# A hybrid decoder step on one core: the norms' sums of squares added up by VectorE in place of GpSimd

## The chip, the cores and the metric

The kernel runs on one core of one Trainium2 chip. The metric is the device time of one execution in microseconds, lower is better; the time before is a median of three runs. The core has a matrix engine (TensorE, PE in the profile, with its weight loads as PEld), three engines for element-wise work (VectorE is DVE, ScalarE is ACT, GpSimd is POOL), and DMA queues, most of them issued by SyncE (SP). Every engine executes its own list of instructions in order and waits on semaphores for the others.

## The reference, cut to what matters

Two layers of a decoder act on 512 prompt tokens and 32 sample tokens of width 1024, all in float32. Every sub-layer starts with an RMS norm and ends with a residual add:

```python
def rms_norm(x, g):
    xf = x.astype(jnp.float32)
    y = xf * lax.rsqrt(jnp.mean(xf * xf, axis=-1, keepdims=True) + RMS_EPS)
    return (y * g.astype(jnp.float32)).astype(x.dtype)
...
    for l in range(DEPTH):
        hp = rms_norm(xp, norm_mix[l])
        # even l: one projection, Mamba-2 heads (whose output is normed too) and window attention
        # odd l: forgetting attention
        ...
        xp = xp + cross_attn(rms_norm(xp, norm_xa[l]), mk, mv, w_xq[l], w_xo[l])
        xp = xp + swiglu(rms_norm(xp, norm_ffn[l]), w_ffn_in[l], w_ffn_out[l])
    y_prompt = rms_norm(xp, norm_final)
```

The sample tokens go the same way. The memory tokens of the cross-attention have a norm of their own. The step also returns states and caches.

## The kernel before, in words

Activations lie transposed: 128 features on the partitions, 8 tiles `k` of features, 544 tokens along the free axis. The tokens are worked in two chunks, `CH`: chunk 0 has 256 tokens, chunk 1 has 288 (256 prompt tokens and the 32 samples). Matrix products keep float32 accuracy by splitting every operand into a high half (a cast on ScalarE, L169, L253, L258) and a low half (a subtraction on VectorE, L170, L256, L259); three matmuls of high and low halves make one product (`acc3`, issued at L138). Weights come through SyncE's queue (L165), and a weight piece feeds 24 matmuls of each chunk. FFN inputs use a second product (L1632) on combined operands built by `operands` and `factors`.

A norm is spread over the projection that ends the sub-layer before. When TensorE has finished one output tile of one chunk, VectorE adds it from PSUM onto the residual `x` (L323; L751 and L752 in the even layer's output projection). Then `norm_tile` makes the high and low halves of `x` times the gain, without the norm's factor, ScalarE squares the tile (L264 for the first tile, straight into the accumulator `acc`; L267 for the others, into one of two `sq` buffers), and GpSimd adds the square onto `acc` (L268). There are seven such adds for each chunk of a norm. After the last tile of a chunk, `rstd` sums `acc` over the partitions with small matmuls against ones, VectorE scales and adds epsilon (L302), GpSimd raises to the power of -1/2 (L303), TensorE spreads the result over the partitions, and VectorE copies it to `b` (L310). The factor `b` is applied only when a product leaves PSUM (L457, L751, L1664 and others), or, in the FFN, when `operands` builds its inputs (L1558).

The line L268 serves seven norms: the norm in front of each cross-attention, of each FFN and of layer 1, the norm of the Mamba output (`gate`, L913), and the final norm, whose last square goes into a tile of its own, `lastsq` (L282), summed by a second matmul; that norm therefore has six adds for each chunk. 6 by 14 and 12 make 96 adds. The first norm of layer 0 (L429) and the memory norm (L1363) do not use this function: their adds stand on VectorE already. The final scaling is L1808, with the stores of `y` behind it (L1811).

In the Mamba scan (`ssm`) GpSimd also works on E (L873), the state (L901), weighted inputs (L854) and outputs (L895), and VectorE on L870, L853, L883 and others; chunk 0 of the Mamba norm falls into it.

The order of the instructions on each engine is laid out by a planner: the program is built under

```python
    with tile.TileContext(nc, schedule_with_timeline_sim=True, auto_bufs=True) as tc, ExitStack() as ctx:
```

so that the program text sets priorities, and the planner's own cost of every instruction decides what comes next on an engine. Some orders are set by hand with `after`, and interleaved by generators in `even` and `odd`.

Of the kernel before, what the change touches and what calls it, by code (L numbers as in the profile page):

```python
# [15 lines left out]
ALU = mybir.AluOpType  # L16
# [90 lines left out]
class Net:  # L107
# [153 lines left out]
    def square_acc(self, acc, src, k, N):  # L261
        nc = self.nc
        if k == 0:
            nc.scalar.activation(acc, src, AF.Square)  # L264
        else:
            sq = self.pers.tile([P, 288], F32, tag="sq", bufs=2, name=self.nm("sq"))
            nc.scalar.activation(sq[:, 0:N], src, AF.Square)  # L267
            nc.gpsimd.tensor_tensor(acc, acc, sq[:, 0:N], ALU.add)  # L268

    def norm_tile(self, st, src, k, c):  # L270
        o, N = CH[c]
# [1650 lines left out]
```

## Time and profile before

| | |
|---|---|
| median of three runs | 1657.58 us (1655.66 to 1658.09) |
| the profiled execution | 1655.56 us |
| its span, first to last instruction | 1653.8 us |
| mean granted TensorE clock | 0.993 |
| TensorE busy | 1623.4 us |
| VectorE busy | 1195.5 us |
| ScalarE busy | 795.2 us |
| GpSimd busy | 310.6 us |
| the 96 adds of L268 on GpSimd | 84.8 us |

Busy times are sums of instructions on one engine; they overlap between engines. A row of a group gives the line, the engine, the operation with its tiles, the count, then busy microseconds, the mean nanoseconds of one, and how long the engine idled just before, with what ended that idling. A row of the time line gives start, length, engine, line and tiles. A row of waits gives who waited for whom, the total, how often, and the longest.

### The profile page before, as it was taken

To read this page: it belongs to the slowest core of one execution; us is meant where nothing else is said; L and a number is where in the kernel's file an instruction comes from. 1 tells how busy PE (TensorE), PEld (TensorE's weight loads), DVE (VectorE), ACT (ScalarE), POOL (GpSimd) and SP (SyncE) were. 2 spreads that over 40 slices of the span, in tenths; PEclk is the share of its full clock that TensorE was granted. 3 is DMA by queue.
4 is the path that set the end of the run, shared out by engine and by line. 5 is a ranking of instruction groups with operands and counts; after the bars stand their busy time and mean duration, and the time that the engine had idled before them with its cause. 6 is when DMAs were issued, how large, how long until landed. Compare 5 with 4: busy or idle time off the path is not lost.

```text
span 1653.8 us, 32422 instructions
## 1 busy us (share of the span) xinstructions
PE 1623.4 (98%) x12720; PEld 1518.6 (92%) x12720; DVE 1195.5 (72%) x2327; ACT 795.2 (48%) x1629; POOL 310.6 (19%) x482
## 2 busy tenths in 40 slices
PE   8999999999999999999999999998999999999998
PEld 7999999878998999999999996656989999999997
DVE  6788789888777877777767478546567986767754
ACT  5467545444445444444435266435445444444434
POOL 0022333763322300000002113111313200000002
PEclk9999999999999999999999999999999999999999
DMA  5221334138342232323213433555441322323222
GB/s 194 65 65 52 123 111 161 40 128 290 119 170 73 66 133 87 106 81 111 86 69 138 143 112 119 173 170 178 147 179 54 122 101 77 115 84 103 77 74 84
DMA packets 71221, 189.27 MB, mean 114 GB/s; under 512 B 7612, under 2 KB 34012, under 8 KB 63452
## 3 DMA queue, kind: packets, MB, share of 16 engines
q1 hardware_dynamic: 69932, 185.43, 33.8%
q8 instruction: 100, 1.64, 0.4%
q10 hardware_dynamic: 1056, 1.24, 0.3%
q0 software_dynamic: 80, 0.52, 0.1%
q14 instruction: 53, 0.43, 0.1%
HBM read 172.22 MB, written 14.95 MB: 113 GB/s over the span
## 4 chain that ended last, share of the span: by engine, by line
PE 73%; DVE 2%; ACT 1%; issue 1%; DMA 0%; POOL 0%; POOLq 0%; DVEq 0%; SPq 0%; ACTq 0%
PE ps L138 48%; PE ps L1632 23%; PE ps L141 2%; DMA fr<-wfi 0%; DVE split_t L170 0%; DVE xn L1573 0%; POOL prt L1210 0%; ACT prt L1198 0%; DVE prt L1197 0%; ACT prt L1321 0%; DVE xf L1568 0%; DVE PT L1180 0%; DVE xpr L1473 0%; ACT split_t L169 0%; ACT PT L1180 0%
## 5 line engine op out<-in xcount | busy, mean ns | idle before, releaser
L138 PE MATMUL ps<-xh,split_t 128*128 128x288 f32 (+1 forms) x2304 | 463.2, 293 | 8.2 <-ACT split_t L169 7.8
L138 PEld LDWEIGHTS ps<-xh,split_t 128*128 128x128 f32 x2304 | 371.0, 190 | 11.2 <-ACT split_t L169 7.8
L1632 PE MATMUL ps<-xf,split_t 128*128 128x272 f32 x2592 | 350.5, 289 | 0.2 <-ACT split_t L1605 0.2
L138 PE MATMUL ps<-xl,split_t 128*128 128x256 f32 (+1 forms) x1152 | 337.9, 294 | 0.0
L1632 PEld LDWEIGHTS ps<-xf,split_t 128*128 128x128 f32 x2592 | 335.7, 188 | 1.1 <-DVE split_t L1606 0.8
L268 POOL TENSOR_TENSOR room<-room,sq 128x256 f32<-128x256 f32 (+1 forms) x96 | 84.8, 888 | 782.4 <-ACT sq L267 781.0
L138 PEld LDWEIGHTS ps<-xl,split_t 128*128 128x128 f32 x1152 | 218.6, 190 | 1.1 <-issue 0.4
L138 PE MATMUL ps<-hh,fs 128*128 128x256 f32 (+1 forms) x1024 | 208.3, 288 | 0.0
L169 ACT CAST split_t<-room 128x1024 fp32r<-128x1024 f32 (+1 forms) x128 | 130.3, 1019 | 136.3 <-PE ps L138 108.3
L170 DVE TENSOR_TENSOR split_t<-room,split_t 128x1024 fp32r<-128x1024 f32 (+1 forms) x128 | 163.8, 1282 | 26.9 <-ACT split_t L169 26.1
L1605 ACT CAST split_t<-fr 128x1024 fp32r<-128x1024 f32 x108 | 113.6, 1052 | 113.2 <-PE ps L1632 49.4
L138 PEld LDWEIGHTS ps<-hh,fs 128*128 128x128 f32 x1024 | 165.7, 188 | 0.0
L1606 DVE TENSOR_TENSOR split_t<-fr,split_t 128x1024 fp32r<-128x1024 f32 x108 | 133.0, 1231 | 42.7 <-ACT split_t L1605 40.0
L138 PE MATMUL ps<-hl,fs 128*128 128x256 f32 (+1 forms) x512 | 147.2, 288 | 0.0
L138 PE MATMUL ps<-oh,split_t 128*128 128x288 f32 (+1 forms) x512 | 102.0, 294 | 0.0
L138 PEld LDWEIGHTS ps<-hl,fs 128*128 128x128 f32 x512 | 96.4, 188 | 0.0
L138 PEld LDWEIGHTS ps<-oh,split_t 128*128 128x128 f32 x512 | 81.6, 190 | 1.8 <-issue 1.8
L138 PE MATMUL ps<-ol,split_t 128*128 128x288 f32 (+1 forms) x256 | 75.3, 295 | 0.0
L138 PE MATMUL ps<-hh,split_t 128*128 128x256 f32 (+1 forms) x384 | 73.5, 289 | 0.0
L1606 DVE TENSOR_TENSOR fs<-fr,fs 128x512 fp32r<-128x512 f32 x36 | 24.9, 691 | 65.1 <-ACT fs L1605 65.1
L258 ACT ACTIVATE xh<-x,room 128x256 fp32r<-128x256 f32 (+1 forms) x96 | 48.1, 517 | 48.9 <-DVE x L323 28.6
L1677 ACT CAST fs<-room 128x512 fp32r<-128x512 f32 x64 | 39.7, 620 | 65.0 <-PE ps L138 56.1
(428 smaller groups left out, 3150.2 us busy)
## 6 DMA issues: line engine op xcount, KB each, us to landing
fr<-wfi SPq DMA_DIRECT2D x36, 1024.0 KB
room<-wfo SPq DMA_DIRECT2D x64, 256.0 KB
room<-wo_e SPq DMA_DIRECT2D x16, 512.0 KB
xk<-mem_k SPq DMA_DIRECT2D x8, 1024.0 KB
xv<-mem_v SPq DMA_DIRECT2D x8, 1024.0 KB
room<-wfi SPq DMA_DIRECT2D x16, 512.0 KB
fox_k<-fox_k SPq DMA_DIRECT2D x64, 128.0 KB
fox_v<-fox_v SPq DMA_DIRECT2D x64, 128.0 KB
```

Source lines behind the costliest of these rows:

```text
L138: return self.placed(self.nc.tensor.matmul(out, lhsT, rhs, start=start, stop=stop))
L141: return self.placed(self.nc.tensor.transpose(out, in_, self.ident[0:k, 0:k]))
L169: nc.scalar.copy(hi[:, 0:n], raw[:, 0:n])
L170: nc.vector.tensor_tensor(lo[:, 0:n], raw[:, 0:n], hi[:, 0:n].bitcast(F32), ALU.subtract)
L258: nc.scalar.activation(hh, src, AF.Copy, scale=g)
L268: nc.gpsimd.tensor_tensor(acc, acc, sq[:, 0:N], ALU.add)
L1605: nc.scalar.copy(hi, t)
L1606: nc.vector.tensor_tensor(lo, t, hi.bitcast(F32), ALU.subtract)
L1632: self.nc.tensor.matmul(ps, w[a][:, k], x[:, b, k], start=start and k == 0 and i == 0, stop=k == 3 and i == 2, skip_group_check=True)
L1677: nc.scalar.copy(hi, raw)
```

## The change

The add of a square onto the accumulator moves from GpSimd to VectorE. The square stays on ScalarE, and the buffers stay as they are.

```diff
@@ def square_acc(self, acc, src, k, N):
         else:
             sq = self.pers.tile([P, 288], F32, tag="sq", bufs=2, name=self.nm("sq"))
             nc.scalar.activation(sq[:, 0:N], src, AF.Square)
-            nc.gpsimd.tensor_tensor(acc, acc, sq[:, 0:N], ALU.add)
+            nc.vector.tensor_tensor(acc, acc, sq[:, 0:N], ALU.add)
```

## The prediction

> **What bounds the kernel now.** I read the page first: its busy shares, its chain, and the group of the instruction that is moved.
>
> ```profile
> span 1653.8 us, 32422 instructions
> ...
> PE 1623.4 (98%) x12720; PEld 1518.6 (92%) x12720; DVE 1195.5 (72%) x2327; ACT 795.2 (48%) x1629; POOL 310.6 (19%) x482
> ...
> PE 73%; DVE 2%; ACT 1%; issue 1%; DMA 0%; POOL 0%; POOLq 0%; DVEq 0%; SPq 0%; ACTq 0%
> ...
> L268 POOL TENSOR_TENSOR room<-room,sq 128x256 f32<-128x256 f32 (+1 forms) x96 | 84.8, 888 | 782.4 <-ACT sq L267 781.0
> ```
>
> TensorE is busy for 98% of the span and carries the chain; the 96 adds are 84.8 us of GpSimd's work, and GpSimd is busy for 19%. So an add matters only where TensorE, or VectorE on its behalf, waits for it. The second view is who TensorE waited for in the whole span, the third who waited for the moved line.
>
> ```profile
> engine line waited for: us in total, times, longest us
> PE ps L138 <- ACT split_t L169: 8.2, 2, 7.8
> ...
> PE ps L138 <- DVE E L870: 1.3, 1, 1.3
> ...
> PE ps L138 <- POOL col L303: 1.0, 1, 1.0
> ...
> PE ps L138 <- ACT lastsq L282: 0.8, 1, 0.8
> ...
> PE ps L138 <- DVE xdt L853: 0.6, 1, 0.6
> ```
>
> ```profile
> who waited for it (us, times):
>   DVE oe L751: 0.7, 1
>   ACT sq L267: 0.5, 1
> ```
>
> TensorE never waited for L268. Its waits are the start (7.8 us), two VectorE results in the state-space scan (1.3 and 0.6 us), the final norm (1.0 and 0.8), and small ones in the odd layer. The reason is in the code: a norm's factor is applied when a projection leaves PSUM, so the projection runs on while the sum is still being made.
>
> **The change part by part.** *Removed:* 96 GpSimd adds (84.8 us). GpSimd's next bound disappears with them: nothing else of the norms runs there but the power L303. *Added:* 96 VectorE adds of the same shapes. The kernel has this very add on VectorE in two places:
>
> ```profile
> L429 DVE TENSOR_TENSOR room<-room,sq x14: 418/436/462, 15.4 to 31.1; 128x256 f32<-128x256 f32 x7, 128x288 f32<-128x288 f32 x7
> L1363 DVE TENSOR_TENSOR kv<-kv,sq x7: 409/410/1002, 270.5 to 288.8; 128x256 f32<-128x256 f32 x7
> 516.14 1.07 DVE L323 TENSOR_TENSOR x<-x,ps 128x256 f32<-128x256 f32 x3
> ```
>
> One add is 0.41 to 0.46 us long; three of the like in a row take 1.07 us, so a row of them costs 0.36 each. 96 by 0.43 is 41 us more of VectorE's busy time, or 35 us packed. *Given back:* VectorE's low-half splits L259 were long while GpSimd added. The groups of 522 to 541 us, and two places without a GpSimd add beside them:
>
> ```profile
> L259 DVE SCALAR_TENSOR_TENSOR xl<-x,room,xh 128x288 fp32r<-128x288 f32 x8 | 6.4, 794 | 0.2 <-ACT xh L258 0.2
> L259 DVE SCALAR_TENSOR_TENSOR xl<-x,room,xh 128x256 fp32r<-128x256 f32 x4 | 2.9, 718 | 0.0
> ...
> 525.21 0.51 DVE L259 SCALAR_TENSOR_TENSOR xl<-x,room,xh 128x288 fp32r<-128x288 f32 x1
> ...
> 455.23 3.50 DVE L259 SCALAR_TENSOR_TENSOR xl<-x,room,xh 128x256 fp32r<-128x256 f32 x7
> ```
>
> 794 against 510 ns and 718 against 500: 8 by 0.284 and 4 by 0.218 make 3.1 us that this stage gets back. That GpSimd is the cause is my inference from the times. The Trainium skill (GPSIMD Engine Reference, section Specifications) says that GpSimd shares its SBUF interfaces with VectorE and contends with VectorE instructions that have two SBUF inputs; the trace agrees, since L259 (two SBUF inputs) is long and L323 (one input from PSUM) is not. That rule also speaks against the change, because the new add has two SBUF inputs itself.
>
> Now stage by stage: VectorE busy in it, and the adds that land in it.
>
> ```profile
> core 0: us, PE busy (x) PEld busy (x) DVE busy (x) ACT busy (x) POOL busy (x), PEclk, DMA share, GB/s
> 300.00:345.00 45.00, 43.09 (x360) 38.13 (x359) 37.19 (x73) 20.29 (x51) 38.69 (x49) 1.00 0.12 36
> ...
> 522.00:541.00 19.00, 19.00 (x156) 19.00 (x155) 17.61 (x29) 14.77 (x29) 11.03 (x12) 1.00 0.31 89
> 1258.00:1276.00 18.00, 18.00 (x149) 18.00 (x148) 15.24 (x26) 12.03 (x26) 12.12 (x13) 1.00 0.41 117
> ```
>
> ```profile
> core 0: us, POOL busy (x), PEclk, DMA share, GB/s
> 300.00:345.00 45.00, 5.33 (x7) 1.00 0.12 36
> ...
> 522.00:541.00 19.00, 10.75 (x11) 1.00 0.31 89
> ```
>
> (1) *Output projections in front of the two FFNs (522 and 1258 us).* 11 adds by 0.36 are 4.0 us, less 3.1 given back: 0.9 us net in a stretch where VectorE has almost no idle time. Who needs it next:
>
> ```profile
> 536.40 0.47 DVE L259 SCALAR_TENSOR_TENSOR xl<-x,room,xh 128x256 fp32r<-128x256 f32 x1
> ...
> 537.87 0.50 PE L138 MATMUL ps<-room 128*128 128x1 f32 x4
> 538.23 0.36 PE L138 MATMUL ps<-xl,split_t 128*128 128x256 f32 x1
> ```
>
> The last split of chunk 0 ends at 536.87 and its matmul starts at 538.23, 1.36 us of cover. The sum's matmul at 537.87 stands ahead of it in TensorE's queue and will need the last VectorE add: 536.87 + 0.41 = 537.28, a cover of 0.6 us. 0.9 less 0.6 leaves 0.3, twice: +0.6. Ends: 0 (the adds fill idle time before 522), and 11 by 0.43 with nothing given back, less 0.6, that is 4.1 each or +8.2 for both.
>
> (2) *Chunk 1 of the state-space norm.*
>
> ```profile
> 411.61 1.96 DVE L259 SCALAR_TENSOR_TENSOR xl<-xs,room,xh 128x288 fp32r<-128x288 f32 x3
> ...
> 414.09 3.33 DVE L259 SCALAR_TENSOR_TENSOR xl<-xs,room,xh 128x288 fp32r<-128x288 f32 x5
> ...
> 417.48 0.40 PE L138 MATMUL ps<-xl,split_t 128*128 128x288 f32 x1
> ```
>
> VectorE ends at 417.42 and TensorE takes the last one at 417.48: no cover. The eight splits take 5.3 us, and 8 by 0.51 would be 4.1: 1.2 back, against 7 adds by 0.36 = 2.5. Net +1.3 at most, -0.3 at best; the later adds can stand behind the splits, so I take +0.5.
>
> (3) *Scan, chunk 0 of that norm (300 to 345 us).* Seven adds: 2.9 us at 0.41, 7.0 if each runs at the 1002 ns of L1363. GpSimd is busy for 38.69 of 45 us here, of which only 5.33 go, and VectorE is already held up beside it:
>
> ```profile
> 314.66 4.98 DVE L913 SCALAR_TENSOR_TENSOR xs<-zs,xs 128x256 f32<-128x256 f32 x4 [0.73 <-POOL xs L895]
> 319.56 1.27 DVE L853 TENSOR_TENSOR xdt<-ps,dt 128x512 f32<-128x512 f32 x2
> ...
> 336.28 5.30 DVE L170 TENSOR_TENSOR split_t<-room,split_t 128x1024 fp32r<-128x1024 f32 x1 [0.41 <-ACT split_t L169]
> ```
>
> These lie in front of TensorE's two waits (0.6 us on L853 and 1.3 us on L870). VectorE idles for 7.8 us of the 45, which takes most of the seven. I take +0.6 (one or two adds ahead of L853); ends -1.9 (both waits go) and +7.0.
>
> (4) *Final norm.*
>
> ```profile
> 1642.17 0.74 POOL room L268
> ...
> 1641.93 2.08 DVE L1808 TENSOR_TENSOR x<-x,ps 128x576 f32<-128x576 f32 x3 [0.64 <-PE ps L138]
> ...
> 1644.26 0.42 DVE L323 TENSOR_TENSOR x<-x,ps 128x256 f32<-128x256 f32 x1 [0.25 <-PE ps L138]
> ```
>
> The last add must now share VectorE with the three scalings of chunk 1 (to 1644.01) and the residual add at 1644.26: 0.41 less the 0.25 between them, +0.1 to +0.2, behind it the square, the sum, the power and the store. Ends -0.3 (0.74 against 0.43) and +0.4. I take +0.1.
>
> (5) *The other norms* (425 to 482, 876 to 916, 1150 to 1200 us): VectorE has slack and TensorE waits for nothing of them; 0, hidden by the projections. Without that cover a norm costs its net VectorE time, about 14 by 0.43 = 6.0 us.
>
> (6) *The wait that is added:* VectorE's add waits for ScalarE's square, and residual adds, weight splits L170 and activation splits L259 stand behind it; TensorE's PSUM banks and operands hang on those. And ScalarE's square waits, with two buffers, for VectorE's add two tiles back, with ScalarE's high halves L258 and weight casts L169 behind it. Before, this second wait was 0.5 us in all. I book 0 beyond (1) to (3), since the planner lays both lists out with these costs in view.
>
> **Sum.** 0.6 + 0.5 + 0.6 + 0.1 = +1.8 us. The profiled execution took 1655.56 us (span 1653.8 and 1.8 around it), so it would become 1657.4. It lies 2.0 under the median of the three runs (1657.58); on that median the forecast is 1659.4, +0.11%. About 0.2% (3.3 us) is what a measurement can tell from no change, so I call it no change.
>
> **The rivals.** *VectorE becomes late (slower).* If the long L259 are not GpSimd's doing, or the adds block on ScalarE's squares for as long as they would save, stage (1) costs up to 4.1 us twice; with (2) and (3) that is +9.4: 1667. Half of it is 1662. It decides from 1.4 us of TensorE idle time in each FFN entry. For it: VectorE's 17.61 of 19 us. Against: VectorE's 1195.5 us over the span leave room, and the residual adds have several PSUM banks in hand.
>
> *The shorter chain pays (faster side, yet within the bound).* An add of 0.43 instead of 0.89 us ends each norm sooner, and without GpSimd beside it the scan's waits go: -1.9, -0.3 and -0.3 give 1655.1. The Trainium skill (GPSIMD Engine Reference, section Engine selection) would send elementwise adds to VectorE, with GpSimd about twice as slow for two inputs. By that the norms' chains shorten, and the chain view bears out only 0.74 us of L268.
>
> *The order is drawn anew.* The planner lays out every engine's list from its own costs, so another engine for 96 instructions can move matmuls far from the norms. The odd layer's and the scan's waits are what it can win or lose: 3.3 to 6 us either way, 1653 or 1662. Nothing in the profile says which.
>
> **How the numbers follow.** No change with the sum above: 0.54 (own range 1655.5 to 1660.9). The shorter chain: 0.08, also no change. VectorE late: 0.17, of which 0.15 beyond the bound. Order drawn anew: 0.21, of which 0.09 slower, 0.10 faster, 0.02 within. Faster 0.10, same 0.66, slower 0.24. The range 1654 to 1665 leaves out the better part of the faster case and the upper end of the late one.
>
> **What would show it.** Right: L1363-like adds of 0.41 to 0.46 us at L268 on VectorE, L259 near 0.5 us at 522 to 541, VectorE's total up by less than 41 us (3.1 returned in each FFN entry alone), TensorE's waits as before. Wrong: TensorE waiting for L268 or L259 in the FFN entries or at 414 us, ScalarE waiting for L268, adds of 1 us in the scan, or matmul orders that differ from before where no norm is.

## The result and the profile after

The changed kernel took 1662.81 us (median of six executions, 1661.21 to 1664.67) beside 1656.57 us of the kernel before: a ratio of 1.0041 with a 95% interval of [1.0029, 1.0054], slower by 0.41%. Timed a second time, beside new executions of the kernel before, it was 1664.90 against 1654.52 us, 1.0058 [1.0042, 1.0074]. The time lies inside the predicted range, but the likeliest case of the prediction, no change, is not what happened.

The first two views are the busy shares of the changed kernel, and the moved line on VectorE with what it waits for and who waits for it.

```profile
PE 1624.1 (98%) x12720; PEld 1518.1 (91%) x12720; DVE 1204.9 (72%) x2423; ACT 795.8 (48%) x1629; POOL 227.9 (14%) x386
```

```profile
L268 DVE TENSOR_TENSOR room<-room,sq x96: 406/444/930, 310.6 to 1652.4; 128x256 f32<-128x256 f32 x48, 128x288 f32<-128x288 f32 x48
...
  ACT sq L267: 8.7, 12
who waited for it (us, times):
  POOL odd L380: 320.1, 1
  ACT eb L892: 5.5, 1
  ACT sq L267: 1.4, 3
```

The adds are what the prediction said they would be: 0.44 us at the median. 96 by 0.444 are 42.6 us, yet VectorE's busy time rose by only 9.4 us (1195.5 to 1204.9). Summed over the two traces, the durations of VectorE's other instructions fell by 23 us: the norms' splits L259 by 20 and the weight splits L170 by 6, while a few others grew. The remaining 10 us are overlap: a busy time counts each instant once (it is not a plain sum of durations), and the adds overlap with their neighbours in VectorE's list. The groups of the first FFN entry (528 to 550 us), kept apart by shape, show the splits:

```profile
L259 DVE SCALAR_TENSOR_TENSOR xl<-x,room,xh 128x288 fp32r<-128x288 f32 x8 | 4.1, 508 | 0.0
L268 DVE TENSOR_TENSOR room<-room,sq 128x288 f32<-128x288 f32 x7 | 3.1, 450 | 0.1
L259 DVE SCALAR_TENSOR_TENSOR xl<-x,room,xh 128x256 fp32r<-128x256 f32 x4 | 1.9, 476 | 0.0
L268 DVE TENSOR_TENSOR room<-room,sq 128x256 f32<-128x256 f32 x4 | 1.7, 415 | 0.0
```

508 and 476 ns where 794 and 718 stood before. TensorE waits nowhere for L268 (GpSimd's 320 us in the rows above is an engine with nothing to do, and ScalarE's 5.5 us at L892 lies in the scan, where TensorE idles less than before). It waits elsewhere, though. These rows of its waits are new or longer:

```profile
PE ps L138 <- DVE CmYi L1011: 3.2, 1, 3.2
...
PE ps L138 <- DVE hb L1006: 1.4, 1, 1.4
...
PE ps L138 <- DVE meml L259: 1.3, 2, 1.1
PE ps L1632 <- ACT split_t L1605: 1.2, 2, 1.0
```

The next view sets the stages side by side, the kernel before first, then the changed one. The columns are the window, its length, the busy time of PE, PEld, DVE, ACT and POOL, TensorE's granted clock, the DMA share and GB/s.

```profile
300.00:360.00 60.00, 58.09 (x463) 50.83 (x462) 47.80 (x94) 25.51 (x59) 46.48 (x59) 0.97 0.18 57
360.00:440.00 80.00, 79.55 (x523) 66.74 (x523) 68.70 (x113) 38.86 (x75) 32.67 (x32) 0.96 0.67 235
520.00:620.00 100.00, 99.83 (x791) 99.20 (x790) 83.46 (x122) 51.03 (x85) 23.57 (x22) 1.00 0.31 98
1060.00:1165.00 105.00, 95.75 (x726) 66.92 (x726) 56.81 (x167) 49.79 (x127) 19.05 (x29) 0.97 0.56 183
1250.00:1350.00 100.00, 100.00 (x797) 99.84 (x796) 86.23 (x124) 52.73 (x90) 25.50 (x25) 1.00 0.30 98
```

```profile
300.00:360.00 60.00, 58.48 (x475) 50.25 (x474) 52.03 (x100) 26.81 (x60) 39.91 (x51) 1.00 0.20 67
360.00:440.00 80.00, 73.83 (x465) 61.98 (x466) 62.93 (x117) 34.09 (x66) 20.68 (x18) 0.91 0.64 220
520.00:620.00 100.00, 98.63 (x777) 97.59 (x777) 82.36 (x138) 50.95 (x90) 12.95 (x10) 1.00 0.28 88
1060.00:1165.00 105.00, 93.67 (x760) 62.89 (x759) 55.18 (x174) 47.94 (x126) 15.73 (x26) 0.97 0.53 169
1250.00:1350.00 100.00, 99.82 (x789) 98.31 (x788) 81.76 (x141) 51.27 (x91) 13.09 (x11) 1.00 0.26 85
```

Two losses can be read from such a row. Window less PE busy is TensorE's idle time, and window times (1 - PEclk) is the time that a lowered clock cost. In the sample part (360 to 440 us) the idle time goes from 0.45 to 6.17 us and the clock's loss from about 3.2 to 7.2 us; the scan before it gains 0.4 and 1.8. The first FFN entry loses 1.2, the odd layer 2.1, the second FFN entry 0.2. The span grew by 9.1 us; the five rows sum to 11.0, since the granted clock is rounded to two digits and part of a slow stretch falls on idle time, where it costs nothing.

**What happens in the sample part.** ScalarE's time line there, before and then after. L999 masks B for one sample, L169 casts a weight piece, L258 makes the high halves of the Mamba output.

```profile
388.12 1.05 ACT L169 CAST split_t<-room 128x1024 fp32r<-128x1024 f32 x1 [1.50 <-DMA room<-wxv]
389.08 0.50 ACT L999 ACTIVATE Bm<-B,room 128x256 fp32r<-128x256 f32 x1
390.67 1.71 ACT L258 ACTIVATE xh<-xs,room 128x256 fp32r<-128x256 f32 x4 [1.09 <-DVE hb L1006]
393.62 1.05 ACT L169 CAST split_t<-room 128x1024 fp32r<-128x1024 f32 x1 [1.24 <-PE ps L138]
394.58 0.51 ACT L999 ACTIVATE Bm<-B,room 128x256 fp32r<-128x256 f32 x1
```

```profile
384.18 0.51 ACT L999 ACTIVATE Bm<-B,room 128x256 fp32r<-128x256 f32 x1
392.82 1.05 ACT L169 CAST split_t<-room 128x1024 fp32r<-128x1024 f32 x1 [8.13 <-DMA room<-wo_e]
394.05 1.04 ACT L169 CAST split_t<-room 128x1024 fp32r<-128x1024 f32 x1 [0.18 <-DMA room<-wo_e]
395.00 0.50 ACT L999 ACTIVATE Bm<-B,room 128x256 fp32r<-128x256 f32 x1
...
398.60 0.49 ACT L999 ACTIVATE Bm<-B,room 128x256 fp32r<-128x256 f32 x1
```

In the changed kernel the casts of the first two pieces of the next projection (wo_e) stand ahead of the last two L999 in ScalarE's list. The first waits 8.13 us for its piece, and everything behind it waits too. On VectorE and then on TensorE the same wait is handed on:

```profile
393.90 1.23 DVE L170 TENSOR_TENSOR split_t<-room,split_t 128x1024 fp32r<-128x1024 f32 x1 [6.48 <-ACT split_t L169]
395.04 1.28 DVE L1006 TENSOR_TENSOR hb<-hb,ps 128x512 f32<-128x512 f32 x2
```

```profile
395.87 0.47 PE L138 MATMUL ps<-X,Bm 128*128 128x512 f32 x1 [1.35 <-DVE hb L1006]
400.08 0.64 PE L138 MATMUL ps<-room,CmYi 128*128 128x32 f32 x2 [3.21 <-DVE CmYi L1011]
```

No add stands in this chain. What changed is the lists that the planner laid out: compared instruction by instruction, TensorE's list differs from before in many places between 316 and 427 us. The odd layer is another matter. From 923 to 1156 us the lists of all five engines are those of before, so its 2.1 us are not a redrawn order; their cause is open.

### The profile page after: what moved, and what is told of

Read it like the earlier page. It is cut to its first block, busy times and chain, and to the rows that moved or that the text cites. A ratio compares the mean times of both kernels' runs of the same rounds, so it can differ in the third digit from the quotient of the medians.

```text
span 1662.9 us, 32378 instructions
## 1 busy us (share of the span) xinstructions
PE 1624.1 (98%) x12720; PEld 1518.1 (91%) x12720; DVE 1204.9 (72%) x2423; ACT 795.8 (48%) x1629; POOL 227.9 (14%) x386
## 4 chain that ended last, share of the span: by engine, by line
PE 87%; DVE 6%; ACT 2%; issue 2%; DMA 2%; POOL 1%; SPq 1%; DVEq 0%; POOLq 0%; ACTq 0%
PE ps L138 61%; PE ps L1632 23%; PE ps L141 3%; DVE split_t L170 1%; DMA room<-wo_e 1%; ACT split_t L169 1%; POOL ft L1666 1%; DMA room<-wxv 0%; DVE xs L913 0%; DVE xn L1573 0%; DVE xl L259 0%; DVE meml L259 0%; SPq L1278 0%; ACT prt L1198 0%; DMA x<-x 0%
## 5 line engine op out<-in xcount | busy, mean ns | idle before, releaser
L169 ACT CAST split_t<-room 128x1024 fp32r<-128x1024 f32 (+1 forms) x128 | 130.4, 1020 | 149.7 <-PE ps L138 93.1
L170 DVE TENSOR_TENSOR split_t<-room,split_t 128x1024 fp32r<-128x1024 f32 (+1 forms) x128 | 157.5, 1232 | 35.3 <-ACT split_t L169 34.3
L303 POOL TENSOR_TENSOR col<-col,room 128x2 f32<-128x2 f32 (+1 forms) x16 | 17.8, 1112 | 620.2 <-DVE col L302 620.2
L1690 DVE TENSOR_TENSOR x<-x,ps 128x288 f32<-128x288 f32 (+1 forms) x128 | 54.0, 431 | 20.1 <-PE ps L138 20.0
L258 ACT ACTIVATE xh<-x,room 128x256 fp32r<-128x256 f32 (+1 forms) x96 | 48.1, 516 | 42.7 <-DVE x L323 21.2
```

Of the source, the lines that this page charges most:

```text
L169: nc.scalar.copy(hi[:, 0:n], raw[:, 0:n])
L170: nc.vector.tensor_tensor(lo[:, 0:n], raw[:, 0:n], hi[:, 0:n].bitcast(F32), ALU.subtract)
L258: nc.scalar.activation(hh, src, AF.Copy, scale=g)
L303: e = nc.gpsimd.tensor_tensor(cc, cc, self.cst[:, C_PW:C_PW + 1].to_broadcast([P, n]), ALU.pow)
L1690: nc.vector.tensor_tensor(x, x, ps, ALU.add)
```

## The experiments

Three theories. **A (order):** the 96 new costs made the planner lay the lists out anew, and the loss is where the new lists leave TensorE idle. **B (work):** the loss is VectorE's own extra work, in proportion to the adds. **A'**, for the FFN entries alone: the sum over a norm stands later in TensorE's list, and the chain behind it (power, factor, operands, weight loads) is late. All variants but two choose the engine per norm, tile or chunk (the helper gets the norm's gain column `g`; its add is then L269, and lines below move by one):

```diff
-    def square_acc(self, acc, src, k, N):
+    def square_acc(self, acc, src, k, N, g=None):
+        eng = nc.vector if CONDITION else nc.gpsimd
...
-            nc.gpsimd.tensor_tensor(acc, acc, sq[:, 0:N], ALU.add)
+            eng.tensor_tensor(acc, acc, sq[:, 0:N], ALU.add)
```

The table gives, for the profiled execution of each, idle time + clock loss by stage, worked out from rows like those above (the granted clock has two digits, so 80 us by 0.01 is a step of 0.8 us; by the records of the clock in the last section, the sample part's 3.2 and 7.2 are 3.4 and 6.8).

| kernel | adds on VectorE | ratio [95%] | scan 300-360 | sample 360-440 | FFN 520-620 | odd 1060-1165 | FFN 1250-1350 |
|---|---|---|---|---|---|---|---|
| before | 0 | 1 | 1.9 + 1.8 | 0.5 + 3.2 | 0.2 + 0 | 9.2 + 3.2 | 0 |
| changed | 96 | 1.0041 [1.0029, 1.0054] | 1.5 + 0 | 6.2 + 7.2 | 1.4 + 0 | 11.3 + 3.2 | 0.2 |
| changed, again | 96 | 1.0058 [1.0042, 1.0074] | 1.4 + 0 | 6.4 + 7.2 | 0.8 + 0 | 11.2 + 3.2 | 1.7 |
| e1_mamba_only | 14 | 1.0056 [1.0040, 1.0071] | 1.6 + 0 | 6.5 + 7.2 | 0 | 12.6 + 5.3 | 0 |
| e2_all_but_mamba | 82 | 1.0020 [1.0011, 1.0030] | 1.9 + 1.8 | 0.5 + 3.2 | 1.5 + 0 | 12.0 + 3.2 | 0.2 |
| e3_pin | 96 | 1.0061 [1.0046, 1.0076] | 1.5 + 0 | 8.8 + 10.4 | 1.2 + 0 | 9.3 + 3.2 | 1.6 |
| e4_mamba_none | 0 | 1.0008 [0.9998, 1.0019] | 1.3 + 3.6 | 0.5 + 3.2 | 0 | 12.8 + 3.2 | 0 |
| m_one | 1 | 1.0005 [0.9992, 1.0017] | 2.3 + 1.8 | 0.5 + 1.6 | 0 | 11.4 + 0 | 0 |
| m_two | 2 | 1.0061 [1.0045, 1.0077] | 1.7 + 0 | 5.8 + 3.2 | 0 | 13.6 + 5.3 | 0 |
| m_three | 3 | 1.0054 [1.0035, 1.0074] | 1.7 + 0 | 6.8 + 7.2 | 0 | 11.8 + 7.3 | 0 |
| m_eleven | 11 | 1.0039 [1.0026, 1.0053] | 1.4 + 0 | 2.3 + 4.8 | 0 | 10.9 + 3.2 | 0 |
| all_but_three | 93 | 1.0054 [1.0036, 1.0072] | 1.4 + 3.6 | 2.3 + 4.8 | 1.0 + 0 | 10.6 + 3.2 | 1.4 |
| ffn_only | 28 | 1.0033 [1.0022, 1.0044] | 1.9 + 1.8 | 0.5 + 3.2 | 1.6 + 0 | 9.7 + 7.3 | 0.2 |
| f_c0 | 14 | 0.9997 [0.9987, 1.0006] | 1.9 + 1.8 | 0.4 + 3.2 | 0 | 9.7 + 5.3 | 0 |

### The Mamba norm alone, and all but it

```diff
+        eng = nc.vector if g == G_SSM else nc.gpsimd      # e1_mamba_only
+        eng = nc.vector if g != G_SSM else nc.gpsimd      # e2_all_but_mamba
```

> VectorE adds up the squares of the state-space (Mamba) norm alone, GpSimd those of all other norms. In the changed kernel the matmuls run 5.5 us late between 377 and 420 us and stay so. Theory A (order): these 5.5 us come from the lists having been laid out differently in the state-space sample part, two wo_e[1] weight pieces and their ScalarE casts standing ahead of the ScalarE copies L999, and this norm alone triggers that: about +5.5 us (ratio 1.0033), all of it lost by 420 us, the offset of the matmuls flat from there, ScalarE idle for about 8 us on the arrival of wo_e near 390 us. Theory B (VectorE's own work): the 14 adds cost what they occupy, at most +1 us (1.0006), and the matmuls before 420 us lose no more than that.

> VectorE adds up the squares of every norm but the state-space one, whose adds stay on GpSimd. Theory A (order in the sample part lost 5.5, the FFN entries 1.75 and 0.7, small ones near 1154 us about 1): nothing lost by 420 us and +3.4 us in all (ratio 1.0021). Theory B (the loss is VectorE's work, spread over all norms by their adds): 82 of 96 adds remain, so about +5.5 us (1.0033), with the offset growing at each norm.

The sample part is settled by this pair: with the Mamba norm's 14 adds alone it loses what the whole change loses there (6.5 + 7.2), and with the other 82 it is as before (0.5 + 3.2). In total e2 is 1.0020, as A had it (1.0021; B 1.0033). e1 is 1.0056, beyond the 1.0033 of A and far beyond B's 1.0006: the odd layer lost as well (12.6 + 5.3 for 9.2 + 3.2). No norm changed its engine there in e1, and 700 us lie between, but TensorE's list differs from before in two stretches of the odd layer, at 1127 to 1150 and 1170 to 1173 us.

### Holding the casts back

The changed kernel, with the loads of the wo_e pieces, and so their casts, ordered behind L999 of sample 6. The order binds the planner alone, no semaphore: in the trace two wo_e loads were issued from 387.70 us, while the casts did come behind that L999, at 398.17 us.

```diff
-            nc.scalar.activation(Bm, B4, AF.Copy, scale=self.blk[:, b:b + 1])
+            bm = nc.scalar.activation(Bm, B4, AF.Copy, scale=self.blk[:, b:b + 1])
+            if b == 6:
+                self.bm6 = bm
...
+                self.whold = self.bm6
                 self.linear(self.pieces(I["wo_e"][1], KD), range(8), KD, yn["h"], yn["l"], ssm_evac, tail=2, lead=3)
+                self.whold = None
```

> The changed kernel with one added constraint: the ScalarE casts of the wo_e[1] weight pieces come no earlier than the ScalarE copy L999 of the sample with index 6, about where they stood before the change. Every add stays on VectorE. Theory A (order): most of the 5.5 us lost between 377 and 420 us comes back, ScalarE's idle time on wo_e near 390 us goes, and the time is about +1 to +2.5 us over before (ratio 1.0006 to 1.0015). Theory B (VectorE's work): the time stays at the changed kernel's 1.0041.

A miss: 1.0061. The pin did not bring the old order back, but made a third one. TensorE's waits (lines below the edits are moved by up to four):

```profile
PE ps L138 <- DVE CmYi L1015: 4.0, 1, 4.0
PE ps L138 <- DVE room L268: 3.4, 1, 3.4
```

Now four L258 stood ahead of L999 in ScalarE's list and did not start before 394.16 us (what they waited for is not settled), so that L999 came at 395.78 us; and later TensorE waited 3.4 us for the adds themselves. So this run does not decide between A and B. What it shows is that another blocked instruction took the place of the first. No run has the 96 adds on VectorE together with the old lists.

### Work taken away

```diff
-            nc.gpsimd.tensor_tensor(acc, acc, sq[:, 0:N], ALU.add)
+            if g != G_SSM:
+                nc.gpsimd.tensor_tensor(acc, acc, sq[:, 0:N], ALU.add)
```

> The kernel before with the adds of the state-space norm left out (that norm's sum of squares then holds only its first tile's squares); all other adds stay on GpSimd. No engine has more to do, GpSimd has 14 adds less. Theory A (order): the lists are laid out anew in the scan and sample part all the same, and the time can move by 2 to 6 us either way although work was only taken away. Theory B (work): between 0 and -2 us (ratio 0.9988 to 1.0000), since the splits beside these adds get a little shorter and nothing gets longer.

1.0008 with an interval across zero: less work, no gain that could be measured, and in the odd layer 12.8 us idle for 9.2 (TensorE's list differs there too). Of the 2 to 6 us that A allowed, the interval leaves room for 2 to 3; B's gain did not show either. One thing this run does settle: with these GpSimd adds gone and nothing put on VectorE, the eight splits L259 of chunk 1 of that norm took 513 ns each, 720 before. So it was GpSimd's adds that had made them long.

### One, two, three adds

One add moved leaves TensorE's list exactly as it was; two or three change it in the scan, the sample part and the odd layer.

```diff
+        eng = nc.vector if g == G_SSM and N == 256 and k == 1 else nc.gpsimd        # m_one
+        eng = nc.vector if g == G_SSM and N == 256 and k in (1, 2) else nc.gpsimd   # m_two
+        eng = nc.vector if g == G_SSM and N == 256 and k < 4 else nc.gpsimd         # m_three
```

> One add only (tile k=1, chunk 0 of the state-space norm) goes to VectorE; TensorE's list then comes out exactly as before. Theory A (order): no change, ratio 0.9990 to 1.0010, with the same idle stretches of TensorE as before. Theory B (VectorE's own work in the scan): 0.4 to 1 us, which this timing cannot tell from nothing either; what would speak for B is a new wait of TensorE on L853 or L870 of over 0.5 us in the scan.

> Two adds only (k=1 and 2, chunk 0 of the state-space norm) go to VectorE. The lists of the scan and of the sample part then come out in a third way, neither that of before nor that of the change: one weight cast and the first high half L258 stand ahead of L999 of the sample with index 6, the others behind. Theory A (order): the time moves by several us, most likely as with three adds, +4 to +10 (ratio 1.0024 to 1.006), with TensorE idle near 395 us and half-clock windows of 3.4 us behind it. Theory B (VectorE's own work): two adds are 0.8 us, ratio 1.0005, not to be told from one add.

> Three adds only go to VectorE: those of the tiles k=1 to 3 of chunk 0 of the state-space norm (they fall into the scan near 320 us); the other 93 stay on GpSimd. With these three the lists of the sample part come out as in the changed kernel, the casts of the first two wo_e[1] pieces ahead of L999 of the sample with index 6. Theory A (order): TensorE idles about 4 us at 394 to 400 us, and the time is +4 to +9 us (ratio 1.0024 to 1.0055; the odd layer's order differs too and can add up to 4). Theory B (VectorE's own work): three adds are at most 3 by 0.41 = +1.2 us, and TensorE waits nowhere that it did not before.

This is the clearest answer of the study. One add: 1.0005 [0.9992, 1.0017]. Two adds, 0.8 us of VectorE's work: 1.0061, as much as all 96. Three: 1.0054. The loss does not grow with the work; it comes with the new list. A new list need not lose, though: e4_mamba_none above and f_c0 below have TensorE lists that differ from before too, at no loss that could be measured. The two lists here lose at different places. With three adds TensorE waits for L1007 and L1012 between 396 and 402 us (L1006 and L1011 of the changed kernel), with two it waits 3.77 us in front of the memory keys and not at 395 us:

```profile
366.73 0.39 PE L138 MATMUL ps<-meml,split_t 128*128 128x256 f32 x1 [3.77 <-DVE meml L259]
```

### All but those three

```diff
+        eng = nc.vector if g == G_SSM and not (N == 256 and k < 4) else nc.gpsimd   # m_eleven
+        eng = nc.vector if not (g == G_SSM and N == 256 and k < 4) else nc.gpsimd   # all_but_three
```

> The other 11 adds of the state-space norm go to VectorE, the three of k=1 to 3 of chunk 0 stay on GpSimd, as do all other norms. The sample part's lists are then those of before. Theory A (order): nothing is lost between 377 and 420 us; 0 to +4 us in all (ratio 1.000 to 1.0024), what there is from the odd layer (1064 to 1155 us), whose order differs. Theory B (VectorE's own work): 11 of the 14 adds, so 11/14 of what the 14 cost (9.3 us), about +7 us (1.0044), lost by 420 us.

> The changed kernel with only the three adds of k=1 to 3 of chunk 0 of the state-space norm back on GpSimd: 93 of 96 adds on VectorE. Theory A (order): the 5.5 us of the sample part return, the FFN entries' 1.75 and 0.7 stay: +2 to +4 us (ratio 1.0012 to 1.0024), TensorE without idle time at 394 to 400 us. Theory B (VectorE's own work): 3% fewer adds, so the changed kernel's +6.5 us stay at about +6.3 (1.0038).

Both came out above what A said (1.0039 for at most 1.0024; 1.0054 for 1.0012 to 1.0024). A was right on its place: no idle time at 394 to 400 us. But as the only cause it fails. With the sample part in its old order, TensorE now meets the chunk 1 adds of the Mamba norm. In m_eleven, TensorE and then VectorE:

```profile
418.72 0.83 PE L138 MATMUL ps<-room 128*128 128x1 f32 x6 [1.78 <-DVE room L269]
```

```profile
416.53 2.13 DVE L269 TENSOR_TENSOR room<-room,sq 128x288 f32<-128x288 f32 x4
```

Four adds in a row end at 418.66 and the sum's matmul starts at 418.72. That is VectorE being late, 1.8 us of idle time and one more slow stretch of the clock at 420 us (4.8 for 3.2 by the row). The changed kernel shows no such wait, and e3_pin one of 3.4 us; why they differ is not shown. all_but_three pays the same there, and the FFN entries (1.0 and 1.4). So what m_eleven's profile places in this part is B in kind, with the reserve that the planner also chose to put these adds behind the splits; and its total (median 1660.78 for 1654.76) is not split further here: its profiled execution was the fastest of nine.

### The FFN entries

```diff
+        eng = nc.vector if g in (G_FFN, G_FFN + 8) else nc.gpsimd                   # ffn_only
+        eng = nc.vector if g in (G_FFN, G_FFN + 8) and N == 256 else nc.gpsimd      # f_c0
```

> VectorE adds in the two FFN norms only (28 of 96); all others on GpSimd. Theory A' (the later sum in the FFN entry delays the operands L1558 and the wfi loads behind them): +1.75 us lost by 607 us and +0.7 by 1330 us, 2.4 in all (ratio 1.0015), plus what the odd layer's order adds (0 to 3). Theory B' (the FFN loss in the changed kernel came from elsewhere, the stage having been entered late): TensorE without idle time at 600 us, ratio 1.000.

> VectorE adds in chunk 0 of the two FFN norms only (14 of 96). In TensorE's list the sum of chunk 0 then stands 9 rows later than before; with both chunks on VectorE (28 adds) it stood 36 rows later and TensorE idled 1.2 us at 596 us. Theory A' (the loss is the sum's place in TensorE's list and the chain behind it: sum, power, factor, operands, weight loads): no idle time of TensorE at 590 to 610 us, nothing lost between 520 and 620 us. Theory B' (VectorE's extra work in the crowded entry): half of the adds, so half of the loss, about 0.8 to 1 us there. The odd layer's order differs as well and can add 0 to 4 us to the total (ratio 1.000 to 1.0025).

The time lines of VectorE, ffn_only and then f_c0 (L303 reads the sum, L311 copies the factor, L1559 builds the FFN's operands; before, L302 stood at 540.49, L310 at 542.28 and L1558 at 548.88):

```profile
539.61 1.35 DVE L269 TENSOR_TENSOR room<-room,sq 128x256 f32<-128x256 f32 x3
544.46 0.16 DVE L303 TENSOR_SCALAR col<-ps 128x2 f32<-128x2 f32 x1 [3.50 <-PE ps L138]
...
548.61 0.42 DVE L311 COPY room<-ps 128x256 f32<-128x256 f32 x1 [1.28 <-PE ps L138]
...
554.56 6.50 DVE L1559 SCALAR_TENSOR_TENSOR xn<-x,room 128x544 f32<-128x544 f32 x8
```

```profile
537.60 0.41 DVE L269 TENSOR_TENSOR room<-room,sq 128x256 f32<-128x256 f32 x1
...
541.03 0.14 DVE L303 TENSOR_SCALAR col<-ps 128x2 f32<-128x2 f32 x1
543.85 0.42 DVE L311 COPY room<-ps 128x256 f32<-128x256 f32 x1 [2.67 <-PE ps L138]
...
550.16 2.77 DVE L1559 SCALAR_TENSOR_TENSOR xn<-x,room 128x544 f32<-128x544 f32 x3
```

In ffn_only the last add ends at 540.96, and VectorE then stands idle for 3.50 us until TensorE makes the sum: in TensorE's list the sum was put 46 matmuls further back by the trace (the expectation has 36 rows), behind products of the FFN. The operands start 5.7 us later; a load of FFN weights waits 6.1 us for them and is issued at 589.65 us, a weight cast on ScalarE waits 2.2 us for such a load, and at 596 us TensorE idles 1.2 us for a weight cast. In f_c0 the sum is 11 matmuls further back (9 rows in the expectation), the operands start 1.3 us later, and no wait of TensorE is left in 520 to 620 us; its ratio is 0.9997. A' held. The second run also speaks against B' as put there (VectorE's extra work), by which half of the loss should have stayed. ffn_only's total (1.0033) is more than the entries explain; the odd layer's clock (7.3 for 3.2) is in its profile.

### The change once more

No edit: the changed kernel as it is.

> The changed kernel, unaltered, a second time, beside the same runs of before. If the cause is the laid-out order, the same idle stretches of TensorE come back to 0.2 us (1.35 and 3.21 us near 395 us, 1.0 at 601 us, 11.3 in 1060 to 1165 us), and the ratio is 1.0035 to 1.0055. If the loss were chance of one execution, the stretches move. The number of half-clock windows of 3.4 us (three to six were seen) may differ and moves the time by 1.7 us each.

The stretches come back where they were: 1.47 and 3.20 us near 395 us, 11.2 in the odd layer. Only the FFN entries moved (0.4 us at 602 and 1.7 at 1329, for 1.0 and 0.2), past the 0.2 us expected. So the sample part's loss is no chance of one execution: it comes back with the lists.

## Why the prediction was right or wrong, point by point

The time lies inside the range of 1654 to 1665, but the forecast, no change at 1659.4, did not come: 1662.81 is 0.41% slower and above the 1660.9 that the no-change case allowed itself. The range holds it because it was widened for the rivals. That the rival that came true, the order drawn anew, had 1662 as a price is luck: it took the price from the waits of the odd layer and the scan, and most of the loss came in the sample part between them.

- **The adds and what they give back:** right, and larger than stated. 0.41 to 0.46 us each; L259 fell to 508 and 476 ns, and VectorE's total rose by 9.4 us of the 41 allowed. That GpSimd had slowed VectorE was an inference; e4_mamba_none, which takes adds away and moves none, now shows it (720 to 513 ns).
- **Step (6), the added waits at 0 "since the planner lays both lists out with these costs in view":** this step failed. The planner did lay the lists out anew, and in the sample part that is where the time went. ScalarE's waits for the adds are 5.5 us in the scan, without harm to TensorE, and 1.4 us at the squares, but weight casts took places in which they block (8.13 us). The rival "the order is drawn anew" described it, had 1662 among its two prices, and got 0.21, less than half of it for slower. By what the runs show it deserved more: two adds suffice to redraw the scan, the sample part and the odd layer.
- **Step (3), scan at +0.6:** the scan itself came out 2.2 us better (0.4 idle, 1.8 clock): the wait for L870 is gone, as the rival of the shorter chain said, and that for L853 grew from 0.6 to 0.9. The sample part behind it, to which the prediction gave no term, lost 9.7 by the same reading.
- **Step (1), FFN entries at +0.3 each:** the term was too small, and by another mechanism. TensorE did not wait for the sum at 537.87; the planner moved the sum back, and the operands were late 50 us on. Idle time of 1.2 and 0.2 us, 0.6 and 1.7 us the second time, within the step's upper bound of 4.1 each.
- **Step (2), chunk 1 of the Mamba norm at +0.5:** not seen in the changed kernel. Where the sample part kept its order, TensorE waited 1.8 us for the add: the rival "VectorE becomes late", above the step's bound of 1.3.
- **Step (4), final norm at +0.1:** nothing there moved (TensorE's waits on L282 and L303 are 0.85 and 1.03 us in both traces, at the end). **Step (5), the other norms at 0:** right in 440 to 520 us; a new wait of 0.5 us on L323 came at 1162 us.
- **The odd layer, read as "small" waits:** a misreading of the waits before. TensorE idled 9.2 us of 105 there, more than in any other stage of the table, and this row stood among its waits:

```profile
PE ps L138 <- DVE ty L1197: 2.8, 2, 2.6
```

- **Not in the prediction at all:** the granted clock (below). Its loss in the sample part went from 3.2 to 7.2 us, more than half as much as the added idle time.

Open: what in the planner's costs tips the order, and what the odd layer's loss comes from. Its idle time was 9.2 us before, and 11.4 in m_one and 11.3 in the changed kernel with the same lists up to 1156 us, so an order worth 2 us cannot be told there from other causes.

## What to carry to other kernels

When a planner lays out the lists, compare them before and after an edit: here the time followed whether and how the list changed (one add, 0; two adds, +0.6%), not the work moved, while two other new lists cost nothing. Freeing an engine of a large sum (23 us of VectorE's time here) gains nothing unless the bound engine was waiting for it. A cast that slips ahead of a recurrence that should precede it can hold up both: here it waited 8.13 us, and TensorE then idled 4.6 us. And an undo that targets one blocked instruction may only bring the next one to the front.

## What the runs showed of the hardware

**TensorE's clock is granted in steps.** In the records of the clock, every slow stretch that begins and ends within a kernel has 0.50 of full speed and lasts 3.41 us or a multiple: 13.65 us at 399 us in the changed kernel, 6.83 us there before. The rows of these stretches, before and then after:

```profile
399.40:406.20 6.80, 6.80 (x40) 6.35 (x40) 6.06 (x16) 1.04 (x1) 0.00 (x0) 0.50 0.80 276
```

```profile
399.10:412.70 13.60, 12.62 (x69) 11.54 (x70) 11.22 (x29) 2.62 (x6) 0.00 (x0) 0.50 0.66 241
```

At half speed, each step of 3.41 us under work costs 1.7 us beside the idle time that came with it. The Trainium skill (TensorE: Matmul & The Clock Gate, section Part 1: The HAM clock gate) describes such a gate: half clock after an idle window, a free-running window of 3413 ns. The steps and the 0.50 agree. Its section HAM oscillation gives as the rule to have no gaps of TensorE over about 3.4 us. Keeping to it was not enough here: half clock came where the longest gaps are 1.35 and 3.21 us around the 13.65 us stretch, and where the kernel before had 6.83 us of half clock after 14 us without a gap. What the gate counts is left open.

This is also most of why executions differ: of 66 executions of the kernel before, timed beside the experiments, the 22 with a mean clock of 0.995 or more took 1653.5 us on average, the 13 with 0.992 or less 1658.1 us. A difference of 2 us between two single traces therefore means little here.
